# Hybrid encoder block on one core: the last quarter of each xbc slab by features, the weighing's blocks in jobs of eight, the exponents a unit later, the gate's first pair split ahead of h's sums

## The chip, the cores and the metric

The kernel runs on one core of a Trainium2 chip. The metric is the device time of one execution in microseconds (us). The median of three runs of the kernel before is 1135.15 us (1134.05 to 1135.17).

## What is computed

One layer of a bidirectional encoder on 256 positions of width 2048, in float32. The lines that matter here, cut from the reference:

```python
hn = rmsnorm(h, mix_norm_pre[i])
proj = hn @ w_in[i]
z, xbc, dt_raw, u = jnp.split(proj, split_at, axis=-1)
y_ssd = ssd_mixer(z, xbc, dt_raw, ...)      # conv, silu, decays exp(seg), scan in two directions
y_pool = pool_mixer(u, pool_w[i], pool_scale[i])
mix = jnp.concatenate([y_ssd, y_pool], axis=-1) @ w_out[i]
h = h + rmsnorm(mix, mix_norm_post[i])
hn = rmsnorm(h, ffn_norm_pre[i])
ff = conv_glu(hn, w_ffn_up[i], ffn_conv_w[i], ffn_conv_b[i], w_ffn_down[i])
h = h + rmsnorm(ff, ffn_norm_post[i])
gate = jax.nn.sigmoid(rmsnorm(h, ple_norm_pre[i]) @ w_ple_gate[i])
h = h + rmsnorm(gate * (p[i] @ w_ple[i]), ple_norm_post[i])
```

Inside the mixer, each chunk of 128 positions has, for each head and direction, a 128 x 128 matrix exp(segment sums) x (C B^T) x dt, which is multiplied into the head's xs.

## The kernel before

Every large product is done in split precision. A float32 tile is cut into a high half (fp32r) and the rest, and three matmuls (high by high, high by low, low by high) add into the same PSUM bank. `split` (L140) does that for a weight tile of 128 x 1024: ScalarE copies the high half (L149), VectorE subtracts it for the low half (L150). High and low halves have five buffers each, the raw weights (1 MB per load, issued on SyncE's queue) three. So the splits may run at most five tiles ahead of TensorE.

The order of the stages is: `dtu` (dt and the pool input), three slabs of `xbc` (slab 2 holds B and C, slabs 0 and 1 hold xs), `z`, `wo` (the output projection, then the sums into h), the feed-forward `ug`/`uv`, `dn` (down, then the sums into h), `ple` and `gt` (the gate). A slab of xbc is done by `feature_major` (L270): four units of four k rows, each unit one load and two split tiles, and for each k row four features with three matmuls of 128 x 256. Four features of 256 positions fill two PSUM tiles, `acc[0]` and `acc[1]`. When both are done, `times_rows` (L364) scales them by the row norm (one DVE instruction each, L367), `conv` (L372) does five taps (one on ACT at L378, four on DVE at L384, for each feature), and tanh (L600) and a product (L602) finish the silu. z is done by `token_major` (L242): eight units of two k rows, 24 matmuls of 128 x 512 each.

Between the units, `aside` (L191) runs the next list of small jobs from `work`, which is written out by hand (L647 to L680), one list for each unit. The jobs are:

- `seg(i)` (L538): two matmuls into two PSUM banks, a copy on ACT (L544), a minimum on DVE (L545), an exponent on ACT (L546). The result lies in the pages E.
- `pool_mix`, `pool_map`, `cb` and `xs_turn`: matmuls into the same two `misc` banks, with ACT and DVE reading them.
- `weigh(t, g)` (L605): 16 scaled blocks of 128 x 128 on ACT (L610), their sum on DVE (L612), the product into E on DVE (L614).
- `far` and `skip` (L619, L624): products of 128 x 1024 on GpSimd, which need all of xs. `mix` (L628): matmuls yo and yd and the sums into y.

The program order gives each instruction a priority, and a scheduler then interleaves the engines' queues by its own estimate of times. So an engine's order isn't simply the written one.

`sublayer` (L725) ends the dn stage: four squares on ACT (L742), four products (L743), the row norms on GpSimd, then for each quarter of the columns two sums into h on DVE (L750) and a `panel_part` (L329): transposes of h on PE, high halves on ACT (L185) and low halves on DVE (L186), which are the gate's stationary operands. After it `ple(1)` is called, and then the gate's `token_major` with its own splits.

Of the kernel before, what the change touches and what calls it, by code (L numbers as in the profile page):

```python
# [13 lines left out]
AF = mybir.ActivationFunctionType  # L14
ALU = mybir.AluOpType

P = 128
L = 256
# [33 lines left out]
def build(nc, a, out):  # L52
# [5 lines left out]
    with tile.TileContext(nc) as tc, \  # L58
# [76 lines left out]
            return xt[0][:, i:i + 1] if i < V_SCW else vt[:, i - V_SCW:i - V_SCW + 1]  # L135


        spare = {}

        def split(name, src, nel, cuts=()):  # L140

# [61 lines left out]
        def seven_products(name, r, a_, acc, alt, start, stop):  # L203

            v = r.rearrange("p (b c) -> p b c", b=4)
            b11 = split(f"{name}a", r[:, :512], 512)
            b2 = split(f"{name}b", r[:, 1024:], 1024)

            nc.vector.tensor_sub(v[:, 0:2], v[:, 1::2], v[:, 0:2])
            nc.vector.tensor_sub(v[:, 3], v[:, 3], v[:, 0])
            nc.vector.tensor_sub(v[:, 2], v[:, 2], v[:, 3])
            t13 = split(f"{name}c", r[:, :1024], 1024)
            t42 = split(f"{name}d", r[:, 1024:], 1024)
            for x, (wh, wl), c, o, own in (
                    ("a11", b11, 0, alt[0], True), ("a12", b2, 0, acc[0][0], False), ("s4", b2, 512, acc[0][1], False),
                    ("s1", t13, 0, alt[1], True), ("s3", t13, 512, alt[2], True), ("a22", t42, 0, acc[1][0], False),
                    ("s2", t42, 512, alt[3], True)):
                xh, xl = a_[x]  # L220
                for q, (xx, ww) in enumerate(((xh, wh), (xh, wl), (xl, wh))):
                    mm(o, xx, ww[:, c:c + 512], own and start and q == 0, own and stop and q == 2)

        def combine(name, acc, alt):
# [14 lines left out]
            add(s165, alt[2], s165)  # L239
            add(acc[1][1], acc[1][1], s165)  # L240

        def token_major(name, w, c0, ks, get, acc, tail=1, fast=(), alt=None, sums=None):  # L242


            group, nu = [], len(ks) // 2
            for u in range(nu):
                k0 = ks[2 * u]
                r = raw(f"{name}r{k0}", w[k0 * P:(k0 + 2) * P, c0:c0 + 1024]
                        .rearrange("(k p) c -> p k c", p=P), 2, 1024)
                if u in fast:  # L250
                    seven_products(f"{name}{k0}", r, sums(k0), acc, alt, u == fast[0], u == fast[-1])
                    continue
                for j in range(2):
                    group.append((k0 + j, *split(f"{name}{k0}_{j}", r[:, j * 1024:(j + 1) * 1024], 1024)))
                if nu - tail <= u < nu - 1:
                    continue

                order = [(t, o, g, q) for t in range(2) for o in columns(acc[t]) for g in group for q in range(3)] \
                    if u == nu - 1 or u - 1 in fast[-1:] else \
                    [(t, o, g, q) for g in group for t in range(2) for q in range(3) for o in columns(acc[t])]  # L260
                for t, (o, c), (k, wh, wl), q in order:
                    xh, xl = (v[:, t * P:(t + 1) * P] for v in get(k))
                    xx, ww = ((xh, wh), (xh, wl), (xl, wh))[q]
                    mm(o, xx, ww[:, c:c + o.shape[-1]], k == ks[0] and q == 0, k == ks[-1] and q == 2)
                if u - 1 in fast[-1:]:
                    combine(name, acc, alt)
                group = []
                aside()

        def feature_major(name, w, c0, get, acc):  # L270

            for u in range(4):
                r = raw(f"{name}r{u}", w[u * 512:(u + 1) * 512, c0:c0 + 512]
                        .rearrange("(k p) c -> p k c", p=P), 4, 512)
                for j in range(2):
                    wh, wl = split(f"{name}{u}_{j}", r[:, j * 1024:(j + 1) * 1024], 1024)
                    for kk in range(2):
                        k = 4 * u + 2 * j + kk
                        xh, xl = get(k)
                        for f in range(4):  # L280
                            s = slice(kk * 512 + f * P, kk * 512 + (f + 1) * P)
                            for q, (ww, xx) in enumerate(((wh, xh), (wh, xl), (wl, xh))):
                                mm(acc[f // 2][:, f % 2 * L:(f % 2 + 1) * L], ww[:, s], xx,
                                   k == 0 and q == 0 and f % 2 == 0, k == NK - 1 and q == 2)
                aside()

        def feature_pairs(name, w, c0, get, acc):
# [306 lines left out]
        def xbc(slab):  # L594
# [7 lines left out]
            nc.vector.scalar_tensor_tensor(cv, th, 1.0, cv, op0=ALU.add, op1=ALU.mult)  # L602
            return cv

        def weigh(t, g):  # L605

            w = page(f"w{t}{g}")
            for d in range(2):
                for h in range(8):
                    nc.scalar.activation(w[:, d * 1024 + h * P:d * 1024 + (h + 1) * P], cbm[:, d, g, t, :], AF.Copy,  # L610
                                         scale=dt[:, t, d * H + 8 * g + h:d * H + 8 * g + h + 1])
            nc.vector.tensor_add(w[:, :1024], w[:, :1024], w[:, 1024:])  # L612
            es = ee[t][:, g * 1024:(g + 1) * 1024]
            nc.vector.tensor_mul(es, es, w[:, :1024])  # L614
# [28 lines left out]
        def job(f, *args):  # L643
# [7 lines left out]
            [job(seg, 0), job(seg, 1)],  # L651
        ])
        bc = xbc(2)
        work.extend([
            [job(seg, 2), job(pool_map, 0), job(pool_map, 1)],
            [job(cb, bc, 0), job(cb, bc, 1), job(seg, 3)],
            [job(seg, 4), job(pool_map, 2)],
            [job(seg, 5), job(pool_map, 3)],
        ])
        xa = xbc(0)  # L660
        work.extend([
            [job(seg, 6)],
            [job(seg, 7)],
            [job(xs_turn, xa, 0), job(weigh, 0, 0)],
            [],
        ])
        xb = xbc(1)
# [1 line left out]


        work.extend([
            [job(weigh, 0, 1)],
            [],
            [job(weigh, 1, 0)],
            [job(xs_turn, xb, 1)],
            [job(weigh, 1, 1), job(far, 1), job(skip, 0), job(far, 0), job(skip, 1)],
            [job(mix, 0, 0)],
            [job(mix, 0, 1), job(mix, 1, 0)],
            [job(mix, 1, 1)],
        ])  # L680
        zacc = [main(f"z{t}") for t in range(2)]
# [40 lines left out]
            load(g, src.partition_broadcast(P))  # L722
            return g

        def sublayer(name, w, ks, get, gain, h, vnext, panel=Panel, fast=((), ()), sums=None):  # L725

            mg = [page(f"{name}m{t}") for t in range(2)]
            sq = [[], []]
            for half in range(2):

                alt = main(f"{name}s{half}") if fast[half] and half == 0 else []
                acc = [main(f"{name}a{half}{t}") for t in range(2)]
                if fast[half]:
                    alt += (main(f"{name}s{half}") if half else []) + [misc(f"{name}s{half}_{i}") for i in (2, 3)]
                token_major(f"{name}{half}", w, half * 1024, ks, get, acc, 1, fast[half], alt, sums)
                for t in range(2):
                    for n in range(2):
                        q = tiny(f"{name}q{t}{half}{n}", 1)
                        junk = sp.tile([P, 512], F32, tag="junk", bufs=1, name=f"{name}j{t}{half}{n}")
                        c = slice(half * 1024 + n * 512, half * 1024 + (n + 1) * 512)  # L740
                        b = acc[t][n]
                        nc.scalar.activation(junk, b, AF.Square, accum_out=q)  # L742
                        nc.vector.tensor_mul(mg[t][:, c], b, gain[:, c])  # L743
                        sq[t].append(q)
            r = [rms(f"{name}{t}", sq[t], 1.0 / D) for t in range(2)]
            pan = panel(f"{name}x")
            for c in range(4):
                s = slice(c * 512, (c + 1) * 512)
                for t in range(2):
                    nc.vector.scalar_tensor_tensor(h[t][:, s], mg[t][:, s], r[t], h[t][:, s],  # L750
                                                   op0=ALU.mult, op1=ALU.add)
                panel_part(f"{name}x", pan, h, vnext, 4 * c, 4 * c + 4)
            return pan
# [70 lines left out]
        def hid_sums(k):  # L824
# [20 lines left out]
            else:  # L845
# [2 lines left out]
            d.update(a11=(h1[:, :P], l1[:, :P]), a12=(h2[:, :P], l2[:, :P]), a22=(h2[:, P:], l2[:, P:]))  # L848
            return d

        hp = sublayer("dn", w_down, list(range(NF)), hid_get, gload("gffn", a["ffn_norm_post"][0]), h, V_PN,
                      fast=((2, 5, 8, 11, 14, 17), (2, 5, 8, 11, 14, 17, 19)), sums=hid_sums)


        pl.append(ple(1))
# [115 lines left out]
```

## Time and profile before

| what | value |
|---|---|
| median of the runs | 1135.15 us |
| profiled execution: time | 1136.76 us |
| profiled execution: span | 1135.0 us |
| PE busy | 1117.3 us (98%) |
| DVE busy | 798.7 us (70%) |
| ACT busy | 630.3 us (56%) |
| mean granted TensorE clock | 0.995 |

The span runs from the first to the last instruction of the profiled execution. Busy time counts the instructions themselves, so an engine's waits are what is missing to the span. A row of the waits gives the engine and line that waited, for whom, and the total, the number and the longest in us. A row of the timeline gives start and duration in us, engine, line, operation, output and inputs, the shape, how many equal ones in a row, and in brackets the idle time before it and what ended it.

### The profile page before, as it was taken

Reading aid. Unit: us, or ns where it says so; the run is one execution under the profiler, and the core shown is the slowest. Engines: PE = TensorE matmul, PEld = TensorE weight load, DVE = VectorE, ACT = ScalarE, POOL = GpSimd, SP = SyncE. Lnnn points to the kernel's source line nnn. Section 1 sums busy time; section 2 is a strip of 40 time slices with the busy share of each in tenths; the row PEclk is TensorE's granted clock in tenths of the full one; section 3 lists DMA queues with packets and bytes.
Section 4 is the critical chain, followed back from the end, with each engine's and each line's share of the span. In section 5 each row is a group of like instructions: output and inputs, shape, how many; then the busy total and the mean of one; then the engine's idle time right before and its main releaser. Section 6 shows DMA issues by size and latency. Waiting matters only on the chain.

```text
span 1135.0 us, 15377 instructions
## 1 busy us (share of the span) xinstructions
PE 1117.3 (98%) x6049; PEld 973.6 (86%) x6049; DVE 798.7 (70%) x1035; ACT 630.3 (56%) x899; POOL 74.4 (7%) x89
## 2 busy tenths in 40 slices
PE   9999999999999999999999999999999999999996
PEld 9998978888888888888888888888888888887885
DVE  6667787754866665665756656668988998898573
ACT  7747693554674545454544545455656656667462
POOL 0200005200110000000000000000000000002001
PEclk9999999999999999999999999999999999999999
DMA  9944437556455555555555556556466646654752
GB/s 365 348 146 140 149 119 261 177 173 200 148 185 191 192 194 193 194 186 186 185 186 190 189 194 195 194 188 223 157 214 223 211 160 223 204 203 149 229 180 74
DMA packets 129591, 219.03 MB, mean 193 GB/s; under 512 B 3696, under 2 KB 96752, under 8 KB 128624
## 3 DMA queue, kind: packets, MB, share of 16 engines
q1 hardware_dynamic: 129232, 217.70, 57.8%
q8 instruction: 47, 0.77, 0.3%
q10 hardware_dynamic: 288, 0.36, 0.1%
q14 instruction: 24, 0.20, 0.1%
HBM read 215.95 MB, written 2.10 MB: 192 GB/s over the span
## 4 chain that ended last, share of the span: by engine, by line
PE 93%; DVE 3%; ACT 2%; issue 1%; POOL 1%; DMA 0%; POOLq 0%; DVEq 0%; ACTq 0%
PE va L86 22%; PE ga L86 21%; PE dna L86 17%; PE woa L86 8%; PE gt L86 7%; PE xbc L86 5%; PE dtu L86 4%; PE z L86 3%; PE dns L86 3%; DVE h L750 1%; PE pw L86 1%; DVE cv L384 1%; PE yd L86 0%; ACT w L610 0%; PE seg L86 0%
## 5 line engine op out<-in xcount | busy, mean ns | idle before, releaser
L86 PE MATMUL ga<-wox,ug_0h 128*128 128x512 f32 x352 | 88.4, 391 | 0.0
L86 PE MATMUL ga<-wox,ug_1h 128*128 128x512 f32 x352 | 87.6, 390 | 0.0
L86 PE MATMUL va<-wox,uv_0h 128*128 128x512 f32 x352 | 87.5, 391 | 0.0
L86 PE MATMUL va<-wox,uv_1h 128*128 128x512 f32 x352 | 86.9, 389 | 0.0
L86 PEld LDWEIGHTS va<-wox,uv_1h 128*128 128x128 f32 x352 | 66.1, 188 | 13.7
L86 PEld LDWEIGHTS ga<-wox,ug_1h 128*128 128x128 f32 x352 | 65.8, 188 | 13.6
L86 PEld LDWEIGHTS va<-wox,uv_0h 128*128 128x128 f32 x352 | 64.7, 188 | 12.5
L86 PEld LDWEIGHTS ga<-wox,ug_0h 128*128 128x128 f32 x352 | 64.5, 188 | 12.2
L86 PE MATMUL dna<-dn_0h,hs 128*128 128x512 f32 x248 | 74.7, 389 | 0.0
L86 PE MATMUL dna<-dn_1h,hs 128*128 128x512 f32 x248 | 74.5, 389 | 0.0
L791 POOL TENSOR_TENSOR fc<-fc,rfb 128x1024 f32<-128x1024 f32 x11 | 26.7, 2426 | 439.2 <-ACT fc L790 439.2
L86 PEld LDWEIGHTS dna<-dn_0h,hs 128*128 128x128 f32 x248 | 46.5, 188 | 9.7
L86 PEld LDWEIGHTS dna<-dn_1h,hs 128*128 128x128 f32 x248 | 46.6, 188 | 9.7
L86 PE MATMUL ga<-wox,ug_1l 128*128 128x256 f32 x352 | 50.3, 284 | 0.0
L86 PE MATMUL ga<-wox,ug_0l 128*128 128x256 f32 x352 | 49.5, 283 | 0.0
L86 PE MATMUL va<-wox,uv_1l 128*128 128x256 f32 x352 | 49.4, 283 | 0.0
L86 PE MATMUL va<-wox,uv_0l 128*128 128x256 f32 x352 | 49.2, 283 | 0.0
L86 PEld LDWEIGHTS ga<-wox,ug_0l 128*128 128x128 f32 x352 | 46.8, 191 | 1.7
L86 PEld LDWEIGHTS va<-wox,uv_0l 128*128 128x128 f32 x352 | 46.7, 191 | 1.7
L86 PEld LDWEIGHTS ga<-wox,ug_1l 128*128 128x128 f32 x352 | 45.7, 192 | 0.2
L384 DVE SCALAR_TENSOR_TENSOR fc<-gr,vt,fc 128x255 f32<-128x255 f32 x88 | 40.3, 481 | 7.8 <-ACT fc L378 7.0
L86 PEld LDWEIGHTS va<-wox,uv_1l 128*128 128x128 f32 x352 | 45.4, 192 | 0.0
(1080 smaller groups left out, 2823.8 us busy)
## 6 DMA issues: line engine op xcount, KB each, us to landing
dn0r<-w_ffn_down SPq DMA_DIRECT2D x22, 1024.0 KB, 5.4
dn1r<-w_ffn_down SPq DMA_DIRECT2D x22, 1024.0 KB, 5.5
zr<-w_in SPq DMA_DIRECT2D x8, 1024.0 KB, 5.3
wo0r<-w_out SPq DMA_DIRECT2D x8, 1024.0 KB, 5.4
wo1r<-w_out SPq DMA_DIRECT2D x8, 1024.0 KB, 5.5
gt0r<-w_ple_gate SPq DMA_DIRECT2D x8, 1024.0 KB, 5.7
gt1r<-w_ple_gate SPq DMA_DIRECT2D x8, 1024.0 KB, 5.6
dtur<-w_in SPq DMA_DIRECT2D x14, 528.0 KB, 8.8
```

What stands on the lines that cost most here:

```text
L86: nc.tensor.matmul(o, lhsT, rhs, start=start, stop=stop, skip_group_check=True)
L384: nc.vector.scalar_tensor_tensor(o[:, lo:hi], i[:, lo + d:hi + d], vec(wcol + j * wstep + f), o[:, lo:hi], op0=ALU.mult, op1=ALU.add)
L750: nc.vector.scalar_tensor_tensor(h[t][:, s], mg[t][:, s], r[t], h[t][:, s], op0=ALU.mult, op1=ALU.add)
L791: nc.gpsimd.tensor_tensor(cv.rearrange("p (f t) -> p f t", f=4), cv.rearrange("p (f t) -> p f t", f=4), rfb.unsqueeze(1).to_broadcast([P, ...
```

## The change

Four edits:

- In `feature_major` the last of the four units goes by features: all matmuls of feature 0 (its four k rows, from both split tiles), then feature 1, and so on. The first three units go by k rows as before.
- `weigh` is cut in two. `scale_by_dt(t, g, d)` makes the eight scaled blocks of one direction, `weigh` only does the sum and the product. The table of jobs places the eights in units of their own, the first two in slab 1 (`xb1`), and moves `xs_turn` of slab 1, `far` and `skip` up in z's units.
- The `seg` jobs begin one unit later.
- `sublayer` takes a function `ahead`, called behind the four products and before h's sums. For dn it splits `ple1`'s tiles and the gate's first two tiles, which `token_major` then takes from `ready`.

```diff
+        def split_two(name, w, k0, c0):
+            r = raw(f"{name}r{k0}", *two_rows(w, k0, c0))
+            return [(k0 + j, *split(f"{name}{k0}_{j}", r[:, j * 1024:(j + 1) * 1024], 1024)) for j in range(2)]
...
-                for j in range(2):
-                    group.append((k0 + j, *split(f"{name}{k0}_{j}", r[:, j * 1024:(j + 1) * 1024], 1024)))
+                group.extend(ready.pop(name) if u == 0 and name in ready else split_two(name, w, k0, c0))
...
+                if u == 3:
+                    for f in range(4):
+                        for j in range(2):
+                            for kk in range(2):
+                                step(j, kk, f)
...
+        def scale_by_dt(t, g, d):
+            if d == 0:
+                ww[t, g] = page(f"w{t}{g}")
+            for h in range(8):
+                nc.scalar.activation(ww[t, g][:, d * 1024 + h * P:d * 1024 + (h + 1) * P], cbm[:, d, g, t, :], AF.Copy,
+                                     scale=dt[:, t, d * H + 8 * g + h:d * H + 8 * g + h + 1])
...
         def weigh(t, g):
-            w = page(f"w{t}{g}")
-            for d in range(2):
-                for h in range(8):
-                    nc.scalar.activation(w[:, d * 1024 + h * P:d * 1024 + (h + 1) * P], cbm[:, d, g, t, :], AF.Copy,
-                                         scale=dt[:, t, d * H + 8 * g + h:d * H + 8 * g + h + 1])
+            w = ww.pop((t, g))
...
-            [job(xs_turn, xa, 0), job(weigh, 0, 0)],
+            [job(seg, 7), job(scale_by_dt, 0, 0, 1), job(weigh, 0, 0)],
...
+            if ahead:
+                ahead()
             r = [rms(f"{name}{t}", sq[t], 1.0 / D) for t in range(2)]
...
+        def gate_ahead():
+            ready["ple1"] = split_two("ple1", w_ple, 0, 1024)
+            ready["gt0"] = split_two("gt0", w_gate, 0, 0)
```

What it moves, at the three places of which the prediction speaks. First ACT, from the copies of slab 0's xs (while slab 1's last unit runs on PE) to the casts of z's third pair. w are the scaled blocks, cv the conv of slab 1, z_0h and z_1h the high halves of a pair. Before:

```order
L592 ACTIVATE xs<-xt_1503 128x512
L610 ACTIVATE w_1509<-cbm,dt 128x128 x16
L610 ACTIVATE w_1652<-cbm,dt 128x128
L378 ACTIVATE cv_1589<-xr_1586,vt 128x256 x2
L610 ACTIVATE w_1652<-cbm,dt 128x128 x3
L378 ACTIVATE cv_1589<-xr_1586,vt 128x256 x2
L610 ACTIVATE w_1652<-cbm,dt 128x128 x12
L149 CAST z_1h<-zr_1671 128x1024
```

And now, from the same copy:

```order
L609 ACTIVATE xs<-xt_1522 128x512
L629 ACTIVATE w_1652<-cbm,dt 128x128 x10
L395 ACTIVATE cv_1589<-xr_1586,vt 128x256 x2
L629 ACTIVATE w_1652<-cbm,dt 128x128
L149 CAST z_1h<-zr_1661 128x1024
L629 ACTIVATE w_1652<-cbm,dt 128x128 x3
L395 ACTIVATE cv_1589<-xr_1586,vt 128x256 x2
L629 ACTIVATE w_1652<-cbm,dt 128x128 x2
```

The 16 blocks of the first weighing are gone from here (they stand in slab 1's first units), and the cast of z's second z_1h stands behind 11 blocks and two conv scales where it stood behind 32 and four.

Second DVE at the same place: xr are the scaled halves of slab 1, E the exponents. Before:

```order
L150 TENSOR_TENSOR z_0l<-zr_1671,z_0h 128x1024
L367 TENSOR_TENSOR xr_1586<-xbc_0_1307,rxb 128x512
L612 TENSOR_TENSOR w_1509<-w_1509 128x1024
L367 TENSOR_TENSOR xr_1586<-xbc_1_1308,rxb 128x512
L614 TENSOR_TENSOR E_639<-E_639,w_1509 128x1024
...
L612 TENSOR_TENSOR w_1652<-w_1652 128x1024
L150 TENSOR_TENSOR z_1l<-zr_1671,z_1h 128x1024
```

And now:

```order
L150 TENSOR_TENSOR z_0l<-zr_1661,z_0h 128x1024
L384 TENSOR_TENSOR xr_1586<-xbc_0_1307,rxb 128x512
...
L384 TENSOR_TENSOR xr_1586<-xbc_1_1308,rxb 128x512
L401 SCALAR_TENSOR_TENSOR cv_1589<-xr_1586,vt,cv_1589 128x254
L401 SCALAR_TENSOR_TENSOR cv_1589<-xr_1586,vt,cv_1589 128x255
L150 TENSOR_TENSOR z_1l<-zr_1661,z_1h 128x1024
```

The low half z_1l stood behind all 16 taps and two sums; it stands behind six taps and no sum.

Third DVE at the end of dn, where dnm are the products, h the sums (dn0r and dn1r are the row norms), dnxl the panel's low halves and gt_0l, gt_1l the gate's first pair. Before, the last lines up to gt_1l:

```order
L150 TENSOR_TENSOR gt_0l<-gt0r_9105,gt_0h 128x1024
L743 TENSOR_TENSOR dnm_7059<-dna_1_8006,gffn 128x512
L750 SCALAR_TENSOR_TENSOR h_2072<-dnm_7058,dn0r,h_2072 128x512
L750 SCALAR_TENSOR_TENSOR h_2073<-dnm_7059,dn1r,h_2073 128x512
...
L186 SCALAR_TENSOR_TENSOR dnxl_8954<-dnxt_8987,vt,dnxh_8952 128x256
L150 TENSOR_TENSOR gt_1l<-gt0r_9105,gt_1h 128x1024
```

And now:

```order
L150 TENSOR_TENSOR gt_0l<-gt0r_8942,gt_0h 128x1024
L766 TENSOR_TENSOR dnm_7059<-dna_1_8006,gffn 128x512
L150 TENSOR_TENSOR gt_1l<-gt0r_8942,gt_1h 128x1024
L775 SCALAR_TENSOR_TENSOR h_2072<-dnm_7058,dn0r,h_2072 128x512
L775 SCALAR_TENSOR_TENSOR h_2073<-dnm_7059,dn1r,h_2073 128x512
```

Only gt_1l moves on DVE: from behind all eight sums and six of the panel's low halves to ahead of the first sum. On ACT at this place the cast of the next pair's gt_1h moves ahead of the first panel part. From z's end to dn's end no engine's order changes.

More of the change, by code (lines that the diff above doesn't have):

```diff
@@ L135, in vec @@
             return xt[0][:, i:i + 1] if i < V_SCW else vt[:, i - V_SCW:i - V_SCW + 1]
-        spare = {}
+        spare, ready = {}, {}
         def split(name, src, nel, cuts=()):
@@ L274, in feature_major, with step @@
                         .rearrange("(k p) c -> p k c", p=P), 4, 512)
-                for j in range(2):
[L276 to L284, printed above, removed]
+                tiles = []
+                def step(j, kk, f):
+                    k = 4 * u + 2 * j + kk
+                    (wh, wl), (xh, xl) = tiles[j], get(k)
+                    s = slice(kk * 512 + f * P, kk * 512 + (f + 1) * P)
+                    for q, (ww, xx) in enumerate(((wh, xh), (wh, xl), (wl, xh))):
+                        mm(acc[f // 2][:, f % 2 * L:(f % 2 + 1) * L], ww[:, s], xx,
+                           k == 0 and q == 0 and f % 2 == 0, k == NK - 1 and q == 2)
+                for j in range(2):
+                    tiles.append(split(f"{name}{u}_{j}", r[:, j * 1024:(j + 1) * 1024], 1024))
+                    if u < 3:
+                        for kk in range(2):
+                            for f in range(4):
+                                step(j, kk, f)
+                if u == 3:
+                    for f in range(4):
+                        for j in range(2):
+                            for kk in range(2):
+                                step(j, kk, f)
                 aside()
@@ L650, in build @@
             [job(pool_mix, 2), job(pool_mix, 3), job(decays), job(seg_sums)],
-            [job(seg, 0), job(seg, 1)],
+            [],
         ])
@@ L654, in build @@
         work.extend([
-            [job(seg, 2), job(pool_map, 0), job(pool_map, 1)],
-            [job(cb, bc, 0), job(cb, bc, 1), job(seg, 3)],
-            [job(seg, 4), job(pool_map, 2)],
+            [job(seg, 0), job(seg, 1), job(pool_map, 0), job(pool_map, 1)],
+            [job(seg, 2), job(cb, bc, 0), job(cb, bc, 1)],
+            [job(seg, 3), job(seg, 4), job(pool_map, 2)],
             [job(seg, 5), job(pool_map, 3)],
@@ L661, in build @@
         work.extend([
-            [job(seg, 6)],
-            [job(seg, 7)],
-            [job(xs_turn, xa, 0), job(weigh, 0, 0)],
+            [job(seg, 6), job(scale_by_dt, 0, 0, 0)],
+            [job(seg, 7), job(scale_by_dt, 0, 0, 1), job(weigh, 0, 0)],
+            [job(xs_turn, xa, 0)],
             [],
@@ L671, in build @@
         work.extend([
[L672 to L678, printed above, removed]
+            [job(scale_by_dt, 0, 1, 0)],
+            [job(scale_by_dt, 0, 1, 1), job(weigh, 0, 1)],
+            [job(xs_turn, xb, 1), job(far, 1), job(skip, 0), job(scale_by_dt, 1, 0, 0)],
+            [job(far, 0), job(skip, 1), job(scale_by_dt, 1, 0, 1), job(weigh, 1, 0)],
+            [job(mix, 0, 0), job(scale_by_dt, 1, 1, 0)],
+            [job(mix, 0, 1), job(scale_by_dt, 1, 1, 1), job(weigh, 1, 1)],
+            [job(mix, 1, 0)],
             [job(mix, 1, 1)],
@@ L723, in gload, with sublayer @@
             return g
-        def sublayer(name, w, ks, get, gain, h, vnext, panel=Panel, fast=((), ()), sums=None):
+        def sublayer(name, w, ks, get, gain, h, vnext, panel=Panel, fast=((), ()), sums=None, ahead=None):
             mg = [page(f"{name}m{t}") for t in range(2)]
@@ L849, in hid_sums @@
             return d
+        def gate_ahead():
+            ready["ple1"] = split_two("ple1", w_ple, 0, 1024)
+            ready["gt0"] = split_two("gt0", w_gate, 0, 0)
         hp = sublayer("dn", w_down, list(range(NF)), hid_get, gload("gffn", a["ffn_norm_post"][0]), h, V_PN,
-                      fast=((2, 5, 8, 11, 14, 17), (2, 5, 8, 11, 14, 17, 19)), sums=hid_sums)
+                      fast=((2, 5, 8, 11, 14, 17), (2, 5, 8, 11, 14, 17, 19)), sums=hid_sums,
+                      ahead=gate_ahead)
         pl.append(ple(1))
```

6 lines of the change are left out of this document (4 added, 2 removed).

## The prediction

> **What bounds the kernel now.** I read the page first, then the waits of PE, then the stretches around the two longest waits, then the order of time on each engine there.
>
> ```profile
> span 1135.0 us, 15377 instructions
> PE 1117.3 (98%) x6049; PEld 973.6 (86%) x6049; DVE 798.7 (70%) x1035; ACT 630.3 (56%) x899; POOL 74.4 (7%) x89
> ```
>
> PE is busy for 1117.3 of 1135.0 us. This change removes no matmul, so it can only win PE's gaps and whatever makes PE slow. The waits of PE (total, times, longest) name the gaps:
>
> ```profile
> PE z L86 <- DVE z_1l L150: 2.5, 1, 2.5
> PE gt L86 <- DVE gt_1l L150: 2.3, 1, 2.3
> ...
> PE seg L86 <- issue: 0.7, 1, 0.7
> ```
>
> The two long ones are the two places that the change touches last: a z tile and a gate tile whose low half DVE splits too late. What they cost beyond the gap stands in the stretches around them (columns: us, then busy time of PE, PEld, DVE, ACT, POOL, then the granted clock and DMA):
>
> ```profile
> 85.02:88.43 3.41, 2.71 (x19) 2.31 (x18) 0.53 (x1) 3.31 (x7) 0.00 (x0) 1.00 0.64 247
> 153.28:156.70 3.42, 0.88 (x5) 0.40 (x4) 3.42 (x5) 3.42 (x9) 0.00 (x0) 1.00 0.00 0
> 156.70:160.11 3.41, 3.41 (x10) 2.65 (x9) 3.41 (x4) 3.41 (x13) 0.00 (x0) 0.50 0.78 246
> 1033.92:1037.34 3.42, 1.13 (x7) 0.76 (x6) 3.42 (x7) 1.57 (x4) 0.00 (x0) 1.00 0.00 0
> 1037.34:1040.75 3.41, 3.41 (x14) 3.02 (x13) 2.63 (x4) 2.20 (x6) 0.00 (x0) 0.50 0.91 279
> ```
>
> After a stretch of 3.41 us in which PE was busy for 0.88 or 1.13 us, the next 3.41 us ran at clock 0.50; after one with 2.71 us busy it stayed at 1.00 (the first row, at the 0.7 us wait). So each long stall is followed by half a window's loss, 3.41 x 0.5 = 1.7 us. The two half-rate windows begin at 156.70 and 1037.34, 880.64 us apart, which is 258 times 3.413: a grid that runs on by itself.
>
> [...]
>
> **The z stall, part by part.** Now ACT has two and a half weighings in a row, and behind them the cast that z needs; DVE has the conv taps and a sum between:
>
> ```profile
> 139.89 5.07 ACT L610 ACTIVATE w<-cbm,dt 128x128 f32<-128x128 f32 x17
> 145.02 1.09 ACT L378 ACTIVATE cv<-xr,vt 128x256 f32<-128x256 f32 x2
> ...
> 147.88 3.61 ACT L610 ACTIVATE w<-cbm,dt 128x128 f32<-128x128 f32 x12
> 151.40 1.04 ACT L149 CAST z_1h<-zr 128x1024 fp32r<-128x1024 f32 x1
> ```
>
> ```profile
> 143.96 0.69 DVE L367 TENSOR_TENSOR xr<-xbc,rxb 128x512 f32<-128x512 f32 x1 [3.68 <-PE xbc L86]
> ...
> 147.58 6.39 DVE L384 SCALAR_TENSOR_TENSOR cv<-xr,vt,cv 128x254 f32<-128x254 f32 x16
> 153.90 1.21 DVE L612 TENSOR_TENSOR w<-w 128x1024 f32<-128x1024 f32 x1
> 155.03 1.21 DVE L150 TENSOR_TENSOR z_1l<-zr,z_1h 128x1024 fp32r<-128x1024 f32 x1
> ```
>
> So one scaled block costs 5.07/17 = 0.30 us on ACT, one tap 6.39/16 = 0.40 us and one full-width DVE operation 1.13 us (start to start, 153.90 to 155.03). PE's own pace in this stage:
>
> ```profile
> 137.85 1.04 PE L591 MATMUL xt<-ident,cv 128*128 128x128 f32 x8
> ...
> 144.47 0.63 PE L86 MATMUL z<-z_0h,hnh 128*128 128x512 f32 x2
> ...
> 152.66 1.09 PE L86 MATMUL z<-z_1h,hnh 128*128 128x512 f32 x4
> 156.30 0.90 PE L86 MATMUL z<-z_1l,hnh 128*128 128x512 f32 x2 [2.54 <-DVE z_1l L150]
> ```
>
> ```profile
> 202.05 0.86 PE yo L86 x2
> 202.91 1.73 PE yd L86 x16
> ```
>
> A z tile takes (152.66 - 144.47)/3 = 2.73 us. I walk the new order on the old clock, with z still beginning at 144.47 (the next part says why). The xb1 slab's last quarter is 48 matmuls between the xt transposes and z. By features, its first PSUM tile is complete after half of them, so about 141.6 instead of about 143.9 (DVE's row above). The first weighing's 16 blocks lie in xb1's first units, at about 121 to 128, where PE's tiles are ready 3 to 5 us ahead, so I cost them at nothing. After the xs copies (139.9) ACT does 10 blocks (142.9), two conv scales (143.9), a block, and casts z_1h at 144.2 to 145.2. DVE does the first xr half (142.4), four taps from 143.4 (145.0), the second half (145.6), two taps (146.4) and then z_1l: ready at 147.5, where PE needs it after 152.66. The stall goes, with 5 us to spare.
>
> What is late next: DVE then has nine taps (151.1), the weighing's sum (152.3), a tap, the product (153.8) and z_0l of the third pair (155.0). PE begins that tile at 144.47 + 4 x 2.73 = 155.4 and asks for the low half two matmuls later, 155.8. This margin, 0.8 us, is the thinnest. After it DVE gains on PE: z_1l at 157.3 against 158.1, the fourth pair's z_0l at 158.4 against 161.9.
>
> GpSimd's four products also move, from the sixth pair to right behind xs, about 163:
>
> ```profile
> 175.53 2.92 DVE L150 TENSOR_TENSOR z_0l<-zr,z_0h 128x1024 fp32r<-128x1024 f32 x1
> ```
>
> ```profile
> 174.49 2.88 POOL L625 TENSOR_TENSOR y<-xs,small 128x1024 f32<-128x1024 f32 x1
> ```
>
> Beside such a product a DVE split takes 2.92 instead of 1.21 us. Four of them cost DVE 6.8 us between 163 and 174. At 163 DVE has split five pairs but for nothing (z_1l of the fifth pair at 161.9, PE needs it at 170); the sixth pair's z_1l, behind sum and product, comes at about 175.6, and PE wants it at 178.1. Cost nothing; if that cover fails, up to 6.8 less the 2.5 of margin. The z term is therefore 2.54 + 1.71 = 4.25 us. A bound above it: the stage 144.47 to 204.64 lasts 60.2 us, and its work (16 tiles of 2.73, 1.0 of xt, four times 0.86 + 1.73 of yo and yd, whose rows from the chain stand above) comes to 55.1, so at most 5.1.
>
> **The exponents and the quarters, earlier.** Here nothing is removed. ACT does the eight mask products and four conv scales before the next cast, and the seg pairs come a unit later, through the same two PSUM banks:
>
> ```profile
> 81.39 0.72 ACT L535 ACTIVATE seg_x<-seg_c,small 32x512 fp32r<-32x512 f32 x1
> ...
> 87.28 0.59 ACT L544 COPY E<-seg 128x512 f32<-128x512 f32 x1
> ```
>
> The mask sums are ready for them at 80.35, as now. Eight products from there end at 86.2, four conv scales at 88.3, three casts at 91.1, and only then is the first seg bank copied (91.7). PE, which is in order, comes to the third seg product at about 90.9 and waits about 0.9 us for that bank, then 0.2 for the next; it no longer waits the 0.7 at 86. Later pairs wait 0.1 to 0.3. By my walk PE reaches 109 and 117 us 0.2 us earlier than before and z at the same time. Term: 0, between 0.7 won and, if one of these waits grows to the size of the two on record with its slow window, 2.5 + 1.7 lost.
>
> **The gate.** DVE has no idle time here but one wait, and the gate tile's low half lies behind the fourth pair of h's sums:
>
> ```profile
> 1026.95 0.74 DVE L750 SCALAR_TENSOR_TENSOR h<-dnm,dn0r,h 128x512 f32<-128x512 f32 x1
> 1028.13 0.75 DVE L750 SCALAR_TENSOR_TENSOR h<-dnm,dn1r,h 128x512 f32<-128x512 f32 x1 [0.44 <-POOL dn1r L326]
> ...
> 1034.35 0.87 DVE L186 SCALAR_TENSOR_TENSOR dnxl<-dnxt,vt,dnxh 128x256 fp32r<-128x256 f32 x2
> 1035.13 1.22 DVE L150 TENSOR_TENSOR gt_1l<-gt0r,gt_1h 128x1024 fp32r<-128x1024 f32 x1
> ```
>
> (In this part times are less 1000.) Moved to 26.95, gt_1l (1.14) fills that 0.44 and delays h's other sums by about 0.6. The 2.29 us stall goes, but new ones come: the cast of the next gt_1h now stands on ACT ahead of the first panel part, so the second part's high half is there at 33.0 and PE, at 32.5, waits 0.55; the third pair of transposes waits for a bank until 37.05 (1.2 us) and the tile after it for its low half until 38.6 (0.6). These sum to 2.4 us but are spread over 6, so I expect the clock to stay. With it PE has done 26 gate matmuls at 41.3, where before it had 24 at 42.7: (42.7 - 41.3) + 2 x 0.23 = 1.85 us won. Bounds: 0.15 if a window still runs at half (1.85 - 1.7), 4.0 if nothing new waits (2.29 + 1.71). Behind it, the following gt_1l is ready about 0.9 us ahead of PE; the stages behind are PE's, so what is won stays.
>
> **The sum.** 4.25 + 0 + 1.85 = 6.1 us, against the profiled execution's 1136.76 us (span 1135.0 and 1.76 around): 1130.7. The median of the runs is 1135.15, 1.6 below the profiled one, about what one half-rate window costs. On a free-running grid a gap of 2.5 us can fall across an edge and leave both windows busy enough; if the timed runs have one slow window less, there is one less to win. With the same windows the median becomes 1129.05, with one less 1130.75; I take the middle, 1129.9.
>
> **The rivals.** A change is measurable here beyond about 0.2%, that is outside 1132.9 to 1137.4.
>
> The gate's clock. With waits of 0.55, 1.2 and 0.6 us between 32.5 and 38.6, the worst 3.41 us hold about 1.6 us of PE work, of which 0.95 are transposes; the trace has a drop at 1.13 and none at 2.71, and nothing between. Then the gate wins 0.15 and the time is about 1131.6. [...]
>
> z's splits still late. If DVE or ACT loses 2 us against my walk (the 0.8 us margin of the third pair), a stall and with it a slow window come back one tile later: 4.25 shrinks to 1 or less, about 1133.6, no measurable change. For it: DVE and ACT are both at 3.42 of 3.42 in the stretch of the stall. Against: the scaled blocks are moved to places with idle time.
>
> Two banks, the slower case. All seg, pool and cb products pass the two PSUM banks, and ACT frees them in its own order. There are seven seg pairs in the two slabs. If each holds PE for over about 1.2 us, and not for 0.1 to 0.9 as walked, 7 x 1.2 = 8.4 us eat the gain and more: 1135.15 - 5.25 + 8.4 = 1138.3. It decides at 1.1 us a pair. Against: the bank's own holders are short (0.59 for the copy).
>
> **How the numbers follow.** Both gains 0.56 (1128 to 1131, at 1129.9); the gate's clock 0.19; z late 0.17; two banks 0.08. Faster: 0.56, 0.19 and a little of the third, 0.77; same 0.16; slower 0.07. The range goes down to 1126.9 (the gate's upper bound of 4.0 with the z stage's 5.1 would be 1126.0) and up to 1133.0, where the late z begins.
>
> **What would show it.** Right: no wait of PE on z_1l, clock 1.00 from 144 to 200, the wo matmuls beginning near 200 instead of 204.64, gate waits under 1.3 us each. Wrong: a wait of PE on a seg bank over 1.2 us, on a z low half, or a 0.50 stretch at the gate.

## The result and the profile after

The changed kernel takes 1128.44 us (median of 4 runs, 1128.12 to 1129.96), the kernel before 1135.02 (4 runs, 1134.05 to 1135.17). The ratio is 0.9946 [0.9929, 0.9964]: faster by about 6 us. The forecast was 1129.9, within 1126.9 to 1133.0.

The page of the changed kernel, its span and busy times, and under it all waits of PE of 0.4 us or more (total, number, longest):

```profile
span 1126.3 us, 15370 instructions
PE 1112.5 (99%) x6049; PEld 969.2 (86%) x6049; DVE 793.1 (70%) x1035; ACT 631.1 (56%) x899; POOL 77.2 (7%) x89
```

```profile
PE dtu L107 <- POOL ident masks.py:199: 1.4, 1, 1.4
PE dnxt L353 <- DVE dnxl L186: 1.2, 1, 1.2
PE woxt L353 <- DVE wox L186: 0.8, 2, 0.4
PE seg L86 <- ACT E L561: 0.7, 1, 0.7
PE rfbp L86 <- DVE rfbw L376: 0.5, 1, 0.5
PE gt L86 <- DVE gt_0l L150: 0.4, 1, 0.4
```

The waits of 2.5 us on z_1l and 2.3 us on gt_1l are gone. New are 1.2 us on dnxl and 0.4 on gt_0l, in the gate. The seg wait has the same size as before, but another releaser: now it is the bank that ACT copies (L561). PE is busy for 1112.5 instead of 1117.3 us with the same 6049 matmuls. Of these 4.8 us, 2.2 lie in the z stage and 1.1 in the last stage, where the half-rate windows were, 1.2 in the front and 0.3 in the slabs.

Where the 8.6 us between the two spans come from is told by the first matmul of each stage in PE's timeline (us; the last stage runs from the first matmul of `ple(1)` to the end of the span). The runs e1 to e10 are those of the next section:

| execution | front, to xbc2 | xbc2 to z | z to woa | woa to ple | ple to end | half-rate windows in z / gate |
|---|---|---|---|---|---|---|
| before | 54.13 | 90.34 | 59.98 | 816.20 | 114.31 | 1 / 1 |
| after | 52.57 | 90.01 | 55.02 | 816.22 | 112.52 | 0 / 0 |
| e1 gate only | 52.72 | 90.38 | 58.39 | 816.23 | 112.50 | 0 / 0 |
| e2 no gate | 52.98 | 89.98 | 55.02 | 816.21 | 114.36 | 0 / 1 |
| e3 features only | 53.08 | 90.21 | 58.43 | 816.21 | 114.33 | 0 / 1 |
| e4 no features | 52.13 | 90.50 | 55.20 | 816.23 | 112.49 | 0 / 0 |
| e5 seg early | 54.49 | 90.16 | 55.02 | 816.22 | 112.49 | 0 / 0 |
| e6 long gap | 52.31 | 90.35 | 62.44 | 816.24 | 114.31 | 2 / 1 |
| e7 gap, matmuls | 52.35 | 90.37 | 61.36 | 816.26 | 112.83 | 0 / 0 |
| e8 gap, transposes | 52.35 | 90.38 | 60.85 | 816.18 | 112.83 | 0 / 0 |
| e9 mixes together | 52.48 | 89.98 | 55.49 | 816.19 | 112.48 | 0 / 0 |
| e10 ahead sooner | 52.09 | 89.99 | 55.05 | 816.29 | 112.54 | 0 / 0 |

The z stage gave 4.96 us, the last stage 1.79, the xbc slabs 0.33. The front gave 1.56, but PE, ACT and DVE run the same instructions in the same order there in all twelve kernels (e7 has one memset more on GpSimd), and it lies anywhere between 52.09 and 54.49: that share isn't the change's. The stage from woa to ple, in which nothing moved, agrees within 0.11 us. So the length of a stage behind the front is a much finer measure here than the time of a run.

The place of the z stall, ACT and then DVE of the changed kernel (start, duration, instruction):

```profile
140.93 1.09 ACT L395 ACTIVATE cv<-xr,vt 128x256 f32<-128x256 f32 x2
141.92 0.40 ACT L629 ACTIVATE w<-cbm,dt 128x128 f32<-128x128 f32 x1
142.21 1.05 ACT L149 CAST z_1h<-zr 128x1024 fp32r<-128x1024 f32 x1
```

```profile
143.87 0.87 DVE L401 SCALAR_TENSOR_TENSOR cv<-xr,vt,cv 128x254 f32<-128x254 f32 x2
144.65 1.22 DVE L150 TENSOR_TENSOR z_1l<-zr,z_1h 128x1024 fp32r<-128x1024 f32 x1
...
150.86 1.23 DVE L637 TENSOR_TENSOR E<-E,w 128x1024 f32<-128x1024 f32 x1
152.00 1.23 DVE L150 TENSOR_TENSOR z_0l<-zr,z_0h 128x1024 fp32r<-128x1024 f32 x1
```

z begins at 142.58 here. z_1l is done 3.3 us later; the walk had 147.5 - 144.47 = 3.0. z_0l of the third pair is done at 153.2, 10.6 us after z's start; the walk had 155.0 - 144.47 = 10.5. PE takes that z_0l at 153.94, so 0.7 us are left; the walk had 0.8. PE had no wait there.

At the gate, DVE and then PE of the changed kernel:

```profile
1019.52 0.68 DVE L766 TENSOR_TENSOR dnm<-dna,gffn 128x512 f32<-128x512 f32 x1
1020.12 1.21 DVE L150 TENSOR_TENSOR gt_1l<-gt0r,gt_1h 128x1024 fp32r<-128x1024 f32 x1
1021.25 0.74 DVE L775 SCALAR_TENSOR_TENSOR h<-dnm,dn0r,h 128x512 f32<-128x512 f32 x1
```

```profile
1030.19 1.06 PE L353 MATMUL dnxt<-ident,h 128*128 128x128 f32 x8 [1.18 <-DVE dnxl L186]
1031.62 0.73 PE L86 MATMUL gt<-gt_0l,dnxh 128*128 128x512 f32 x2 [0.37 <-DVE gt_0l L150]
```

gt_1l now fills the time in which DVE waited for the row norms. The third group of transposes waits 1.18 us, and the tile after it 0.37 for its low half.

### The profile page after: what moved, and what is told of

It is laid out like the page before. It is cut to its first block, busy times and chain, and to the rows that moved or that the text cites. A ratio compares the mean times of both kernels' runs of the same rounds, so it can differ in the third digit from the quotient of the medians.

```text
span 1126.3 us, 15370 instructions
## 1 busy us (share of the span) xinstructions
PE 1112.5 (99%) x6049; PEld 969.2 (86%) x6049; DVE 793.1 (70%) x1035; ACT 631.1 (56%) x899; POOL 77.2 (7%) x89
## 4 chain that ended last, share of the span: by engine, by line
PE 95%; ACT 2%; DVE 1%; issue 1%; DMA 0%; POOL 0%; DVEq 0%; POOLq 0%; ACTq 0%
PE va L86 22%; PE ga L86 21%; PE dna L86 17%; PE woa L86 8%; PE gt L86 7%; PE xbc L86 6%; PE dtu L86 4%; PE z L86 4%; PE dns L86 3%; PE pw L86 1%; PE yd L86 1%; DVE h L775 0%; PE ple L86 0%; PE seg L86 0%; DMA dtur<-w_in 0%
```

## The experiments

The theory: each part pays in its own stage. z gives the stall, the half-rate window behind it and something more; the gate gives its stall and window less the new waits; the early part gives nothing.

**e1: the gate's part alone.** The kernel before with `ready`, `split_two` and `ahead=gate_ahead` of the change's diff, nothing else.

```diff
+            if ahead:
+                ahead()
...
-                      fast=((2, 5, 8, 11, 14, 17), (2, 5, 8, 11, 14, 17, 19)), sums=hid_sums)
+                      fast=((2, 5, 8, 11, 14, 17), (2, 5, 8, 11, 14, 17, 19)), sums=hid_sums,
+                      ahead=gate_ahead)
```

> The kernel before with the gate's split alone moved ahead of h's sums. Theory (each part pays for itself in its own stage): the stage from the first ple matmul to the end of the span falls from 110.0 us to about 108.0 as in the changed kernel, the z stage (first z to first woa matmul) stays near 60 us with its wait of 2.5 us on z's low half (58.5 if the half-rate window doesn't follow it in this execution), and the time is about 2 us below the kernel before, 1133. Rival (the parts help each other, or the gate's gain was chance of that execution): the last stage stays within 0.7 us of 110.0 and the time within 1 us of before.

The expectations of e1 and e2 count the last stage from the second matmul of `ple(1)`, 4.3 us later than the table does: their 110.0 us are the table's 114.31, and e1 has 108.19 by that count.

Measured: last stage 112.50, z stage 58.39 with the wait of 2.5 us on z_1l and no half-rate window. The time is 1133.21 us against 1134.20, ratio 0.9982 [0.9973, 0.9991], so 1 to 3 us faster. The theory holds, and the z stage gives the price of a window: 59.98 - 58.39 = 1.59 us. Why there was none here, the same gap cut by the clock's 3.413 us grid shows. The grid's edge is read from the clock's record in the trace, which begins on it: in before's record each of the two half-rate windows lasts 3.413 us, and in all four executions with such windows, the time from the record's beginning to each window is a whole number of 3.413 us (43 and 301 in before).

```profile
150.71:154.13 3.42, 1.68 (x8) 1.02 (x6) 3.42 (x7) 3.42 (x6) 0.00 (x0) 1.00 0.00 0
154.13:157.54 3.41, 2.62 (x12) 2.18 (x13) 3.41 (x4) 3.41 (x13) 0.00 (x0) 1.00 0.43 103
```

An edge fell into the gap, and each of the two windows kept 1.68 and 2.62 us of PE work.

**e2: the change without the gate's part.**

```diff
-                      fast=((2, 5, 8, 11, 14, 17), (2, 5, 8, 11, 14, 17, 19)), sums=hid_sums,
-                      ahead=gate_ahead)
+                      fast=((2, 5, 8, 11, 14, 17), (2, 5, 8, 11, 14, 17, 19)), sums=hid_sums)
```

> The changed kernel without the gate's split ahead. Theory: the z stage is 55.0 to 55.2 us as in the changed kernel, the last stage goes back to 108.3 to 110.1 us (a wait of 2.3 us on gt_1l comes back, with or without a half-rate window of 1.7 behind it), and the time is 1.0 to 2.0 us above the changed kernel, about 1130, so 4 to 5 us below before. Rival (the gate gave nothing): last stage and time as in the changed kernel, 108.0 and 1128.4.

Measured: z stage 55.02, last stage 114.36, time 1129.84 us (ratio to before 0.9953 [0.9941, 0.9966]), 1.4 above the changed kernel. As the theory has it. Here the gate's gap had its window, after 1.39 us of PE work:

```profile
1026.25:1029.67 3.42, 1.39 (x11) 1.01 (x9) 3.42 (x6) 2.54 (x5) 0.00 (x0) 1.00 0.00 0
1029.67:1033.08 3.41, 3.16 (x12) 2.76 (x13) 2.23 (x5) 0.47 (x1) 0.00 (x0) 0.50 0.52 160
```

**e3 and e4: which of the z edits removes the stall.** e3 is the kernel before with the last quarter by features alone; e4 the changed kernel with that quarter by k rows.

```diff
-                if u == 3:
-                    for f in range(4):
-                        for j in range(2):
-                            for kk in range(2):
-                                step(j, kk, f)
```

(Cut from e4's diff, which puts the old loops over k rows back for all four units; e3 makes the reverse edit in the kernel before.)

> The kernel before with the last quarter of each slab by features alone. Theory: ACT still makes 32 scaled blocks ahead of the cast of the second z_1h, and DVE two sums, so the wait on z_1l stays at 2 to 2.6 us, the z stage at 58.4 to 60.2 us, and the time within 1 us of before. Rival (the features bring the gain by letting the conv begin 2.3 us sooner): the wait falls under 0.5 us and the z stage to about 56 us.

> The changed kernel with the last quarter of each slab by k rows as before. Theory (the split of the weighing does it): no wait on z_1l of the second pair. The conv begins about 2 us later, and z_0l of the third pair, now behind 16 taps, a sum and a product, is ready at about the time PE asks for it: a wait there of 0 to 1.5 us, the z stage at 55.0 to 56.5 us, the time at most 1.5 us above the changed kernel. Rival (the features are needed): a wait of 2 us or more in z with a half-rate window behind it, z stage 58 us or more.

Measured: e3 keeps a wait of 2.6 us on z_1l, z stage 58.43, time 1133.86 (ratio 0.9993 [0.9984, 1.0002]): no change. The first scaled half xr begins 2.7 us ahead of z there and 0.5 in the kernel before, but ACT still does 16 blocks ahead of the first conv scale, and the taps begin 3.1 us after z's start in both. e4 has no wait in z, z stage 55.20, time 1128.43, the changed kernel's. So the table of jobs removes the stall, and the order by features does little for the time: 0.2 us in the z stage and 0.5 in the slabs (90.50 against 90.01) between e4 and the changed kernel. In e4 the third pair's z_0l, the thinnest margin of the walk, still comes in time, but only just:

```profile
152.73 1.22 DVE L150 TENSOR_TENSOR z_0l<-zr,z_0h 128x1024 fp32r<-128x1024 f32 x1
```

It is ready at 153.95 and PE takes it at 154.00, where the changed kernel has 0.7 us left. What the features buy in z is this margin. (In e4 DVE also makes the second pair's z_1l ahead of all taps, so its order isn't only the changed kernel's with a later conv.)

**e5: the exponents in their old units.**

```diff
-            [],
+            [job(seg, 0), job(seg, 1)],
         ])
         bc = xbc(2)
...
-            [job(seg, 0), job(seg, 1), job(pool_map, 0), job(pool_map, 1)],
-            [job(seg, 2), job(cb, bc, 0), job(cb, bc, 1)],
-            [job(seg, 3), job(seg, 4), job(pool_map, 2)],
+            [job(seg, 2), job(pool_map, 0), job(pool_map, 1)],
+            [job(cb, bc, 0), job(cb, bc, 1), job(seg, 3)],
+            [job(seg, 4), job(pool_map, 2)],
```

> The changed kernel with the seg jobs in the units where they stood before. Theory (the exponents' place brings and costs nothing): the stretch from the first xbc2 matmul to the first z matmul stays at 89.9 us within 0.5, and the time within 1 us of the changed kernel. Rival (the later place is what lets the scaled blocks run in slab 1's first units): a wait of PE of over 1 us there or in z, and the time 1.5 us or more above the changed kernel.

Measured: slabs 90.16, z 55.02, time 1128.49 (ratio 0.9946 [0.9929, 0.9963]). The later place of the exponents is worth 0.15 us. In the slabs e5 differs from e3 by the first weighing, which it has in slab 1's first units; that makes 0.05 us (90.16 against 90.21). Leaving these aside, e3 and e4 complete the slabs' four cases: neither edit 90.34, the features alone 90.21, the later exponents alone 90.50, both 90.01. No wait on the two banks is longer than 0.9 us (e4) in any order.

**e6, e7, e8: does the idle PE make the half-rate window, and do transposes keep the clock as matmuls do?** In the kernel before, DVE computes z's second z_1l twice, so that the gap no longer depends on the grid. e7 fills the gap with 24 matmuls that add zero, e8 with 42 transposes into banks that nobody reads.

```diff
+                for _ in range(2 if name == "z2_1" else 1):
                     last["dve"] = ins(nc.vector.tensor_sub(lo[:, s], src[:, s], hi[:, s].bitcast(F32)))
...
+                        for i in range(24):
+                            fill = mm(acc[0][0], zero, wh[:, :512], False, False)
```

(The second piece in e7; e8 has `nc.tensor.transpose` there, 21 for each of two banks.)

> The kernel before with the low half of z's second z_1 tile computed twice on DVE, so that the gap of PE grows from 2.5 to about 5.9 us wherever the grid of the clock stands. If a gap makes the half-rate window: one or two windows of 3.41 us at clock 0.50 behind it, the z stage at 60.2 + 3.4, so 63.6 us with one window, 65.3 with two.

> The same kernel with the longer gap, and in it 24 matmuls of 128 x 512 with a stationary operand of zeros into z's own bank (they add zero), 5.5 us of PE. If idle PE makes the half-rate windows: no 0.50 window in z, and the z stage about 1.7 us shorter for each window that the longer gap alone had. If the windows have another cause, such as what ACT and DVE do there: the same windows as without the filling.

> The same kernel with the longer gap, and in it 42 transposes of 128 x 128, about 5.5 us of PE. If transposes keep the clock as matmuls do: no 0.50 window in z, as with the matmuls. [...]

Each was run once: 1137.44, 1135.11 and 1134.37 us. The long gap unfilled, on the grid of its own execution:

```profile
150.99:154.40 3.41, 0.94 (x5) 0.43 (x3) 3.41 (x7) 3.41 (x7) 0.00 (x0) 1.00 0.00 0
154.40:157.81 3.41, 1.94 (x8) 1.57 (x8) 3.41 (x5) 3.41 (x13) 0.00 (x0) 0.50 0.00 0
157.81:161.23 3.42, 3.32 (x8) 2.66 (x9) 3.42 (x5) 3.42 (x8) 0.10 (x1) 0.50 0.60 178
161.23:164.64 3.41, 3.41 (x17) 2.78 (x16) 3.41 (x5) 3.06 (x9) 3.41 (x1) 1.00 1.03 411
```

Two windows at 0.50. The z stage is 62.44, not 63.6 or 65.3: the scheduler put eight xt transposes into the gap, and in the first half-rate window PE waited anyway for 1.5 of the 3.41 us. With the matmuls there is no window, and the z stage is 61.36, shorter by 1.1 us. That is less than the 3.4 expected for two windows, since one was hidden in the wait and since e7 has four of the eight xt transposes still to do behind the gap (0.5 us). With the transposes there is none either, and the z stage is 60.85. First PE's timeline of e8, then its windows:

```profile
151.39 4.75 PE L269 MATMUL fill<-ident,z_1h 128*128 128x128 f32 x42
155.90 0.71 PE L86 MATMUL z<-z_1h,hnh 128*128 128x512 f32 x2
156.44 1.03 PE L600 MATMUL xt<-ident,cv 128*128 128x128 f32 x8
157.96 0.73 PE L86 MATMUL z<-z_1l,hnh 128*128 128x512 f32 x2 [0.48 <-DVE z_1l L151]
```

```profile
153.14:156.55 3.41, 3.41 (x32) 3.28 (x30) 3.41 (x4) 3.41 (x12) 0.00 (x0) 1.00 0.00 0
156.55:159.96 3.41, 2.93 (x18) 2.35 (x17) 3.41 (x4) 3.41 (x8) 0.00 (x0) 1.00 0.24 40
```

In the window from 153.14, all but the 0.54 us from 155.90 to 156.44 are transposes. Without them PE has less work there, 0.54 us, than in any window that was followed by 0.50 (0.88 at the least), and yet the clock stayed at 1.00. So here the half-rate window goes with the idle PE (in the two grid windows from e6's 150.99, e7's 151.33 and e8's 149.72 on, ACT and DVE are busy throughout, 3.41 or 3.42 us in each), and with these transposes in the gap the clock stayed at 1.00 as with the matmuls. In e6 the first z_1l matmul starts at 157.91 and in e8 at 157.96, behind the same xt transposes: what differs after it, 62.44 - 60.85 = 1.59 us, is again one window.

**e9: the mixes back together.**

```diff
-            [job(mix, 0, 0), job(scale_by_dt, 1, 1, 0)],
-            [job(mix, 0, 1), job(scale_by_dt, 1, 1, 1), job(weigh, 1, 1)],
-            [job(mix, 1, 0)],
+            [job(scale_by_dt, 1, 1, 0)],
+            [job(mix, 0, 0), job(scale_by_dt, 1, 1, 1), job(weigh, 1, 1)],
+            [job(mix, 0, 1), job(mix, 1, 0)],
```

> The changed kernel with the four mixes in the units where they stood before: the first in z's sixth unit, two together in the seventh, one in the last. The z stage fell by 5.0 us, of which the stall is 2.54 and the half-rate window 1.6; in two runs that kept the stall without the window the stage was 58.4, so 3.4 above the changed kernel's 55.0, and 0.85 of that is not the stall. Theory: the 0.85 us are waits of yo and yd for the sums into y between two mixes of one unit; the z stage rises to 55.6 to 56.0 us, with waits of PE on y or ym of 0.2 to 0.5 each, and the time by 0.6 to 1.0 us. Rival: they come from elsewhere in z (ACT and DVE running later throughout), and the z stage stays at 55.0 within 0.2.

Measured: z stage 55.49, 0.47 above the changed kernel, less than the 55.6 to 56.0 expected; time 1128.64, 0.2 above, where 0.6 to 1.0 were expected. One wait came back, the one the kernel before also had:

```profile
188.93 2.00 PE L86 MATMUL yd<-xs,E 128*128 128x64 f32 x16 [0.19 <-DVE y L664]
```

So the spread mixes are about half of the 0.83 us in z that are neither stall nor window; but the waits of the theory are only 0.19 of these 0.47 us, and in the rest PE is busy for longer, for a reason that stays open. The other 0.36 us have no wait of their own in the trace of e1; part of it is its eight xt transposes, which took 1.2 us in all where the changed kernel's took 1.0. The rest stays open.

**e10: the gate's split ahead of the products.** An attempt at a faster version.

```diff
+                if ahead and half:
+                    ahead()
                 for t in range(2):
                     for n in range(2):
                         q = tiny(f"{name}q{t}{half}{n}", 1)
...
-            if ahead:
-                ahead()
```

> The changed kernel with the gate's split called ahead of the four products instead of behind them, as an attempt at a better version. Theory (DVE is full from 1010 to 1033 us, so order alone wins nothing there): the waits of 1.2 us on dnxl and 0.4 on gt_0l stay within 0.3 in sum, the last stage at 112.5 us within 0.4, the time that of the changed kernel. Rival (the order still matters): the waits fall below 1.0 in sum and the last stage below 112.0.

Measured: waits 1.2 and 0.4 as before, last stage 112.54, time 1128.13 (1127.75 to 1128.57), which overlaps the changed kernel's runs. DVE is nearly full there (busy for 16.49 of the 17.07 us from 1016.26 to 1033.33), and its order wins nothing more.

## Why the prediction was right

- **z.** The stall went, as walked, with the margins as walked (3.3 against 3.0 us and 10.6 against 10.5). The term was 4.25 us, with 5.1 as the bound from the stage less its work; measured 4.96. It consists of 2.54 of stall, 1.59 of window (1.71 forecast) and 0.83 that the term left out and only the bound held: 0.47 of it are the mixes. The table of jobs did it (e4). That the scaled blocks are its working part is read from ACT's order, in which the cast stands behind 11 blocks (8 in e4) instead of 32; no run separates them from the other jobs that the table moves. The order by features, which the walk counted as 2.3 us of head start for the conv, wasn't needed for the stall; alone it gave the conv no head start (e3), and in the changed kernel it gives the third pair its margin. The 32 blocks are two weighings, not two and a half as the prediction has it; the walk counts them rightly. GpSimd's products at nothing: right, PE is busy for all 55.02 us of z.
- **The exponents and the quarters.** The term was 0; measured 0.33 us won, which needs both edits (e3 wins 0.13, e4 loses 0.16). The wait on the first seg bank came, 0.7 instead of 0.9, and the old wait went. The rival of the two banks, which needed 1.1 us a pair, fell.
- **The gate.** The term was 1.85; measured 1.79. The waits were forecast at 1.2 and 0.6 and measured at 1.18 and 0.37; the one of 0.55 on the high half isn't among the waits shown. But what the 1.85 is made of, the runs tell more exactly: with the old gap and without a window the last stage is 112.83 (e7, e8), so the split itself wins 0.3 us and the window's absence 1.5. That the size came out is in part luck. The new waits are 1.55 us where 2.4 were forecast, which leaves 0.7 of the old stall of 2.29 as won; but PE's busy time grows by 0.4 (102.18 against 101.79 in e7 and e8), which the prediction didn't have and no run explains. The rival (a window at half rate also in the new order) rested on 1.6 us of PE work in the worst window. In the six executions with the split ahead (the changed kernel, e1, e4, e5, e9, e10) the worst window held 1.96 (e9) to 2.60 us, and none was followed by 0.50.
- **The half-rate windows.** The step "after a stretch with 0.88 or 1.13 us busy the next runs at 0.50, with 2.71 it doesn't" was right, and so was the doubt whether each run has both windows. Of three executions with the old z gap one had a window (the profiled one of before; e1 and e3 not), of six with the old gate gap four (before, e2, e3, e6; e7 and e8 not). So the two windows that the sum removes are not there in every execution.
- **The sum.** 6.1 forecast against the profiled execution, 8.6 measured there: 4.96 + 1.79 + 0.33 = 7.1 from the change and 1.56 from the front. For the timed runs the number of windows counts, and the granted clock of each run tells it: in the profiled executions 0.997 and 0.998 go with no window in z and at the gate, 0.996 with one, 0.995 with two, 0.993 with three. Of the 35 runs of the kernel before that were timed beside e1 to e10, 18 have 0.996 (1133.37 to 1134.20 us) and 17 have 0.995 or 0.994 (1134.20 to 1137.17); the changed kernel's runs have 0.997 or 0.998. (The stretch at 0.50 behind the last matmuls, 5.5 us in before and 4.4 in the changed kernel, shifts these figures, by an estimate from such stretches up to 0.001, so a single run may be counted wrongly.) That makes about one and a half windows a run, and 3.4 of z without a window (58.4 - 55.0), 0.3 of the gate, 0.3 of the slabs and 1.5 times 1.5 for the windows make 6.3 us. The means, 1134.70 of these 35 runs and 1128.74, differ by 6.0; the medians by 5.8 (21 runs of e1's comparison) to 6.6 (the first four).
- **One window less.** This step of the sum was not borne out. The 1.6 us between the profiled execution and the median were put down to a window, but the 10 runs between 1134.80 and 1135.51 have the clock of two windows. So have the profiled one and the six runs from 1136.69 to 1137.17. What sets the profiled one apart is its long front (54.13 us; ten of the twelve executions have 52.09 to 53.08). So the median, 1135.15, most likely had both windows, and the same sum without the step gives 1129.05, nearer to the measured 1128.44 than 1129.9. That is still 0.6 us too high, and the terms had left out more than this, 0.83 us in z and 0.33 in the slabs.

## What to carry to other kernels

A gap of PE of 2.3 to 2.5 us cost itself here and, depending on where the clock's grid cut it, another 1.5 us; scattered waits of 1.2 us and less, at the gate, brought no half-rate window. So look for the longest gap rather than for the sum of the waits. When a stall is an instruction that is late on a full engine, ask which block of work ahead of it has slack and cut that into small pieces; whether its own input comes sooner may not matter. And compare stages, each from a first instruction to the next stage's first: here those behind the front repeat within 0.1 us between kernels that have the same code and windows there, where whole runs of one kernel differ by 2 and more.

## What the runs showed of the hardware

The clock. PE's busy time in one 3.413 us window of the grid and the granted clock of the next, for all windows in z and at the gate that began at full rate and held under 2 us:

| PE busy in the window, us | execution, place | next window |
|---|---|---|
| 0.88, 1.13 | before, z and gate | 0.50 |
| 0.94, 1.36 | e6, z and gate | 0.50 |
| 1.12 | e3, gate | 0.50 |
| 1.39 | e2, gate | 0.50 |
| 1.68 | e1, z | 1.00 |
| 1.70 | e8, gate | 1.00 |
| 1.81 | e7, gate | 1.00 |
| 1.96, 1.99 | e9, gate; e3, z | 1.00 |

Two rows for the two sides of the edge, from e6 and e8:

```profile
1035.04:1038.45 3.41, 1.36 (x9) 1.18 (x10) 3.41 (x7) 1.16 (x3) 0.00 (x0) 1.00 0.08 12
1038.45:1041.87 3.42, 3.42 (x12) 2.84 (x11) 3.06 (x6) 3.06 (x8) 0.00 (x0) 0.50 0.88 286
```

```profile
1033.77:1037.19 3.42, 1.70 (x12) 1.53 (x13) 3.42 (x6) 1.13 (x3) 0.00 (x0) 1.00 0.19 26
1037.19:1040.60 3.41, 3.41 (x18) 2.55 (x17) 3.34 (x7) 3.41 (x9) 0.00 (x0) 1.00 0.83 286
```

In these rows the most work ahead of a window at 0.50 is 1.39 us and the least ahead of one at 1.00 is 1.68, 41 and 49% of the window (by the trace's busy time, in which the ends of matmuls are modelled). The windows in which PE's work ends, near the end of the span, fit: after 0.11 (before), 1.31 (e8), 1.36 (e1) and 1.37 us (e2) the next is at 0.50, after 1.93 (e10) and 2.48 us (the changed kernel) it is at 1.00. Of the windows in z and at the gate that were at 0.50 themselves, one in e6 with 1.94 us of busy time was followed by another at 0.50; the other six, with 3.16 (e2) to 3.42 us, were followed by 1.00.

The front of the kernel, with the same code everywhere, took 52.09 to 54.49 us. That is more than the gate's part is worth. The two long fronts, 54.13 in before and 54.49 in e5, are those in which the clock's record begins late, at 9.92 and 10.77 us; in the ten others it begins between 4.21 (e6) and 7.35 (e1). Ahead of it the matmuls run at about half the pace in before (0.29 us apart against 0.16), though the views print 1.00 there. Two stretches of before, then the same two of the changed kernel, whose record begins at 5.74 (the number of PE's matmuls in a microsecond stands behind its busy time):

```profile
7.00:8.00 1.00, 1.00 (x5) 1.00 (x5) 0.83 (x2) 0.69 (x2) 0.00 (x0) 1.00 0.99 360
8.00:9.00 1.00, 1.00 (x5) 1.00 (x4) 1.00 (x3) 0.91 (x2) 0.00 (x0) 1.00 1.03 418
```

```profile
7.00:8.00 1.00, 1.00 (x8) 1.00 (x7) 0.00 (x0) 0.56 (x1) 0.00 (x0) 1.00 0.94 330
8.00:9.00 1.00, 1.00 (x8) 0.92 (x6) 0.74 (x1) 1.00 (x3) 0.00 (x0) 1.00 1.01 414
```

In before 14 matmuls of dtu run at the slower pace, which makes about 1.9 us in all. The spread of 1.0 us among the ten short fronts stays open.
